# Gating values of a decoder trunk: token-major products of 256 columns become feature-major products with transposes

## The chip, the cores and the metric

One core of a Trainium2 chip runs the whole kernel in one launch. The metric is the device time of that core in microseconds, the median of several runs. One further run was taken with the profiler; all rows below come from it.

## The reference

The kernel computes one layer of a hybrid decoder for 2048 tokens of width 1024, all in float32. Cut to what the change touches:

```python
h = modulate(rms_norm(x, g_mix[l]), shift1, scale1)
proj = h @ w_in[l]                        # 1024 -> 2*512 (z_a: u|v) + 512 q + 128 k + 128 v
out_a = chunked_sgu(jax.nn.gelu(z_a), w_spatial[l], b_spatial[l])
out_b = sliding_window_sink_attention(q, k, v, sinks[l], positions)
x = x + gate1 * (concatenate([out_a, out_b], axis=-1) @ w_out[l])
...                                       # adaLN, squared-ReLU MLP of width 4096, final RMSNorm

def chunked_sgu(z, w_s, b_s):             # 8 groups x 64 channels, chunks of 128 tokens
    u, v = jnp.split(z, 2, axis=-1)
    v = v.reshape(B, n_chunks, CHUNK, GMLP_GROUPS, HEAD_DIM)
    w = w_s * causal[None]
    sv = jnp.einsum('hts,bcshd->bcthd', w, v) + jnp.transpose(b_s)[None, None, :, :, None]
    return u * sv.reshape(B, S, GMLP_WIDTH)
```

The gating contracts v over the tokens of a chunk, so its matmul wants v with tokens on the partitions. u only multiplies the result element by element, with features on the partitions.

## The kernel before

**Tiling.** The tokens are worked in four slabs of T = 512 (slab 0 to 3), D = 1024 in KT = 8 tiles of 128. Every product is made of float32r parts: an operand is split into a high part (a copy on ACT) and a low part (a subtraction on DVE), and a product is hi·hi + hi·lo + lo·hi, three matmuls per tile (`mm3`, L323 to L328). A projection of 128 output features for one slab is a `group` (L330): 8 tiles × 3 = 24 matmuls of 512 columns into one PSUM bank.

**Buffers.** PSUM has eight banks in four rings: `mm` (3 banks, the groups), `sc` (2: scores and the gating sums `so`), `pt` (2: transposes of attention and of v, and others), `ov` (1). In SBUF `wk` is a ring of 12 tiles of 128 × 1024 that holds weight blocks: raw weights, their high and low parts, and the MLP's tiles `w2w`, `w2h`, `w2l`, `aw`, `ah`, `al`.

**Weights.** `w_take` (L316) loads a weight block when it is first asked for; several keys load the next ones too. In slab 0 a block of `w_in` comes in raw (`raw`), ACT and DVE split it (L293, L294), and both parts are written to DRAM (`ki3h`, `ki3l` for block i3). Later slabs read those parts back (`whi<-ki2h`, `wlo<-ki2l`). All these transfers are issued by SP's queue in program order: writes are put in a list by `put` and sent when loads (`get`) come after them.

**The gating, `in_vu` (L514).** For a pair of feature tiles, `tokens(pp)` takes two weight blocks and makes v token-major: the 128 × 128 tile of h is the stationary operand and 256 weight columns are the moving one (L537 to L539), 4 token blocks × 8 tiles × 3 = 96 matmuls of 256 columns. Then come gelu on ACT (`vf`, L525), a copy to the high part (`vt`, L543) and a subtraction to the low part (L544). The u groups follow (24 matmuls of 512 columns each), then `gate(p)` (L548): 12 matmuls `so` on the parts of v (L557 to L559) and the additions on DVE (L562). The weight blocks are i0, i1 (v of p = 0, 1), i2, i3 (u0, u1), i4, i5 (v of p = 2, 3), i6, i7 (u2, u3). Each u group asks only for its own block.

**Order.** The program is written as generators that are woven together, and a scheduler unrolls it to one fixed order per engine. `in_vu` runs woven with the making of slab 1's h in slab 0; with slab 0's attention in slab 1; with `h2_build` (norm and MLP input of tokens of slabs 0 and 1) in slab 2; and as a side job of the first MLP pass `ffn_d(0)` (L1225 to L1251) in slab 3. In `Stat`, `finish` makes four column sums on TensorE (`msp`, L229), POOL and DVE make the diagonal factors `dg`, and `cast` spreads them with two matmuls `bcp` (L249), whose copy `rbc` (L251) starts the long DVE chain that makes h.

Of the kernel before, what the change touches and what calls it, by code (L numbers as in the profile page):

```python
# [11 lines left out]
F32 = mybir.dt.float32  # L12
F32R = mybir.dt.float32r
I32 = mybir.dt.int32
AF = mybir.ActivationFunctionType
ALU = mybir.AluOpType

P = 128
D = 1024
KT = D // P  # L20
# [3 lines left out]
NB = T // P  # L24
# [25 lines left out]
def hybrid_block(ctx, tc, x_l, c_l, pos, wada0, wada, vec, win, wsT, bs, sinks, wout, w1, w2, rope_c, y_l):  # L50
    nc = tc.nc
    pe, act, dve, pool = nc.tensor, nc.scalar, nc.vector, nc.gpsimd
# [4 lines left out]
    ps = ctx.enter_context(tc.tile_pool(name="ps", bufs=1, space=bass.MemoryType.PSUM))  # L57

    def t2(name, dt=F32, shape=None):
        return sb.tile(shape or [P, T], dt, name=name, tag="t2", bufs=NT)  # L60

    def m2(name, dt=F32R, shape=None):
        return sb.tile(shape or [P, T], dt, name=name, tag="m2", bufs=NM)
# [11 lines left out]
    def put(dst, out, in_):  # L75

        pend.append([0, dst, out, in_])
# [10 lines left out]
    def get(out, in_, src=None):  # L88

        known = [i for i, p in enumerate(pend) if p[1] is src]  # L90
        if src is not None and known:
            emit(known[-1] + 1)
        ins = nc.sync.dma_start(out=out, in_=in_)  # L93
        if not hold[0]:
            for p in pend:
                p[0] += 1
            emit(sum(p[0] > 1 for p in pend), ins)
        return ins
# [4 lines left out]
    def bank(tag="mm", name="mm"):  # L103
        return ps.tile([P, T], F32, name=name, tag=tag, bufs={"mm": 3, "sc": 2, "pt": 2, "ov": 1}[tag])


    ident = const.tile([P, P], F32, name="ident")
# [164 lines left out]
    last_mm = [None]  # L272
# [35 lines left out]
    def w_load(key):  # L308
        if key not in kept:
            return w_split(key)  # L310
        hi, lo = wk("whi"), wk("wlo")
        for t, d in zip((hi, lo), kept[key]):
            get(t.bitcast(F32), d, d)
        return Split([hi], [lo])

    def w_take(*keys):  # L316

        for key in keys:
            if key not in ready:
                ready[key] = w_load(key)  # L320
        return ready.pop(keys[0])

    def mm3(out, wh, wl, h, first, last, more=False):  # L323

        kw = dict(skip_group_check=True) if more else {}
        pe.matmul(out=out, lhsT=wh, rhs=h[0], start=first, stop=False, **kw)  # L326
        pe.matmul(out=out, lhsT=wh, rhs=h[1], start=False, stop=False, **kw)  # L327
        last_mm[0] = pe.matmul(out=out, lhsT=wl, rhs=h[0], start=False, stop=last, **kw)  # L328

    def group(rhs, *keys):  # L330
        w = w_take(*keys)
        out = bank()
        n = len(rhs)
        for k in range(n):
            mm3(out, *w.cut(k * P, (k + 1) * P), rhs[k], k == 0, k == n - 1)
        return out
# [177 lines left out]
    def in_vu(s, h, st, u0=None):  # L514
        vts, us = {}, {}
        sgu = list(wsp)
        if s > 0:
            ts = [m2("wsp", F32R, [P, 4, P]) for _ in range(4)]
            for t, d in zip(ts, wspd):
                get(t.bitcast(F32).rearrange("p g c -> p (g c)"), d, d)  # L520
            sgu = [ts[0:2], ts[2:4]]

        def gelu(bank, name):
            t = t2(name)
            act.activation(out=t, in_=bank, func=AF.Gelu_apprx_tanh)  # L525
            return t

        def tokens(pp):
            w = w_take(("i", 4 * pp), ("i", 4 * pp + 1)), w_take(("i", 4 * pp + 1))
            for half in range(2):  # L530
                o = bank()
                ov = o.rearrange("p (b c) -> p b c", b=2)
                for b in range(2):
                    cols = slice((2 * half + b) * P, (2 * half + b + 1) * P)
                    for k in range(KT):
                        hi, lo = w[k // 4].cut((k % 4) * 2 * P, (k % 4 + 1) * 2 * P)
                        pe.matmul(out=ov[:, b], lhsT=h[k][0][:, cols], rhs=hi, start=k == 0, stop=False)  # L537
                        pe.matmul(out=ov[:, b], lhsT=h[k][1][:, cols], rhs=hi, start=False, stop=False)
                        last_mm[0] = pe.matmul(out=ov[:, b], lhsT=h[k][0][:, cols], rhs=lo, start=False,  # L539
                                               stop=k == KT - 1)  # L540
                vf = gelu(o, "vf")
                vh, vl = m2("vt"), m2("vt")
                act.activation(out=vh, in_=vf, func=AF.Copy)  # L543
                dve.tensor_tensor(out=vl, in0=vf, in1=vh, op=ALU.subtract)  # L544
                vts[pp, half] = tuple(t.rearrange("p (b c) -> p b c", b=2) for t in (vh, vl))
                yield

        def gate(p):  # L548
            u = us.pop(p)
            sv = t2("sv")  # L550
            cols = slice((p % 2) * P, (p % 2 + 1) * P)
            w_h, w_l = (t[:, 2 * (p % 2):2 * (p % 2) + 2] for t in sgu[p // 2])
            for half in range(2):
                vh, vl = vts[p // 2, half]
                so = ps.tile([P, 2, 2, P], F32, name="so", tag="sc", bufs=2)
                for i in range(2):
                    pe.matmul(out=so[:, i], lhsT=vh[:, i, cols], rhs=w_h, start=True, stop=False)  # L557
                    pe.matmul(out=so[:, i], lhsT=vl[:, i, cols], rhs=w_h, start=False, stop=False)
                    pe.matmul(out=so[:, i], lhsT=vh[:, i, cols], rhs=w_l, start=False, stop=True)  # L559
                for hh in range(2):  # L560
                    r0, r1 = hh * HD, (hh + 1) * HD
                    dve.tensor_tensor(out=sv[r0:r1, half * 2 * P:(half + 1) * 2 * P].rearrange("p (c t) -> p c t", c=2),  # L562
                                      in0=so[r0:r1, :, hh, :],
                                      in1=bsb[r0:r1, p, :].unsqueeze(1).broadcast_to([HD, 2, P]), op=ALU.add)
            dve.tensor_tensor(out=sv, in0=sv, in1=u, op=ALU.mult)
            put(mixd[s][p], mixd[s][p], sv)

        for pp in range(2):
            for _ in tokens(pp):
                if pp and 1 in us:  # L570
                    gate(1)
                yield
            for p in (2 * pp, 2 * pp + 1):
                us[p] = u0 if p == 0 and u0 is not None else gelu(group(h, ("i", 4 * (p // 2) + 2 + p % 2)), "u")
                if p % 2:
                    gate(p - 1)
                if p > 0 or u0 is None:
                    yield
        gate(3)
        yield  # L580


# [550 lines left out]
    h, fed = [], [0] * NPRE  # L1133
# [27 lines left out]
    with tc.issue_after(ahead[0].ins):  # L1161
        setup_mixers()
        rope_load(0)
        st = sts[0]
        va_rest = do_va(0, bva, st)
        u0 = t2("vf")
        act.activation(out=u0, in_=bv0, func=AF.Gelu_apprx_tanh)
        va_rest()
        do_k(0, bk, st)
        for j, b in enumerate((bq0, bq1, bq2, bq3)):  # L1170
            do_q(0, j, b, st)
        rb, hn = [], []
        ada = chain(ada_rest(2), ada_rest(3), ada_rest(4))
        weave(in_vu(0, h, st, u0), chain(x_stats(1, rb), spread(rb), h_build(1, rb, hn)), per=2)
# [19 lines left out]
    def then_halo(s, g):  # L1194
# [5 lines left out]
    st1 = sts[1]  # L1200
    mix, mix1, rn, hx = [], [], [], []
    weave(chain(in_qkv(1, hn, st1), in_vu(1, hn, st1)),
          ratio(chain(then_halo(0, attention(0, st)), mix_build(0, mix)), 3,
                chain(part(ada, 6), x_stats(2, rn), spread(rn)), 1), per=3.5)
# [8 lines left out]
    next(h2)  # L1213
    next(h2)
    weave(in_vu(2, hx, sts[2]), h2, per=1.5)
    run(h2)
    w2f, ada = w2_early(), ada_rest(5)
# [98 lines left out]
```

## Time and profile before

| | before |
|---|---|
| runs, median (lowest to highest) | 2097.52 us (2090.8 to 2101.14), 3 runs |
| the profiled run, its span | 2087.11 us, 2085.4 us |
| TensorE (PE) busy | 1917.2 us (92%), 8852 matmuls |
| VectorE (DVE) busy | 1419.1 us (68%) |
| ScalarE (ACT) busy | 914.2 us (44%) |
| main DMA queue | 67.5% of 16 engines' span |
| mean granted PE clock | 0.967 |

The profiled run is 10.4 us below the median of the runs shown. PE, DVE, ACT, POOL and SP are the engines; PEld is TensorE's loading of the stationary operand, which lies beside its matmuls. SPq is the queue on SP that issues transfers. In a row of the timeline the bracket tells how long the engine sat idle before the instruction and what released it. Consecutive matmuls overlap in the pipe, so what one costs in a stream is the distance between starts, not its recorded duration.

### The profile page before, as it was taken

To read this page: it belongs to the slowest core of one execution; us is meant where nothing else is said; L and a number is where in the kernel's file an instruction comes from. 1 tells how busy PE (TensorE), PEld (TensorE's weight loads), DVE (VectorE), ACT (ScalarE), POOL (GpSimd) and SP (SyncE) were. 2 spreads that over 40 slices of the span, in tenths; PEclk is the share of its full clock that TensorE was granted. 3 is DMA by queue.
4 is the path that set the end of the run, shared out by engine and by line. 5 is a ranking of instruction groups with operands and counts; after the bars stand their busy time and mean duration, and the time that the engine had idled before them with its cause. 6 is when DMAs were issued, how large, how long until landed. Compare 5 with 4: busy or idle time off the path is not lost.

```text
span 2085.4 us, 25949 instructions
## 1 busy us (share of the span) xinstructions
PE 1917.2 (92%) x8852; PEld 1581.0 (76%) x8852; DVE 1419.1 (68%) x2400; ACT 914.2 (44%) x1565; POOL 170.9 (8%) x234
## 2 busy tenths in 40 slices
PE   5899898988999999889979979989999999999997
PEld 4788776777877788668867757767888888888875
DVE  8578789648776765784565675794766665544674
ACT  3435644334443444633443344543454444433442
POOL 4301312100000000110101120000000000000000
PEclk9999999999999999889989999999999999999998
DMA  9797497982577857797577778675444446556663
GB/s 318 295 354 249 146 347 236 356 324 101 202 270 249 268 174 247 249 323 254 204 271 248 241 261 313 237 257 162 172 152 162 155 153 208 193 200 210 234 214 129
DMA packets 236214, 486.77 MB, mean 233 GB/s; under 512 B 23809, under 2 KB 81281, under 8 KB 236081
## 3 DMA queue, kind: packets, MB, share of 16 engines
q1 hardware_dynamic: 234960, 484.38, 67.5%
q8 instruction: 70, 1.15, 0.2%
q0 software_dynamic: 1120, 0.72, 0.1%
q14 instruction: 64, 0.52, 0.1%
HBM read 349.55 MB, written 135.46 MB: 233 GB/s over the span
## 4 chain that ended last, share of the span: by engine, by line
PE 47%; DMA 9%; DVE 6%; ACT 2%; issue 1%; SPq 1%; POOL 0%; POOLq 0%; DVEq 0%; ACTq 0%
PE mm L327 15%; PE mm L328 15%; PE mm L326 15%; DMA aw<-ad 3%; DMA xt<-in_x_dram 1%; DVE al L70 1%; DMA w2w<-in_w_dram 1%; DMA xt<-x2d 1%; ACT ah L69 1%; DVE w2l L70 1%; DMA w2w<-w2d 1%; DMA xt<-mixb 1%; SPq L93 1%; DVE x L950 1%; DMA w2d<-a 1%
## 5 line engine op out<-in xcount | busy, mean ns | idle before, releaser
L327 PE MATMUL mm<-al,w2h 128*128 128x512 f32 x896 | 356.0, 397 | 12.6 <-DVE al L70 12.2
L328 PE MATMUL mm<-ah,w2l 128*128 128x512 f32 x896 | 352.9, 394 | 0.0
L326 PE MATMUL mm<-ah,w2h 128*128 128x512 f32 x896 | 313.8, 402 | 24.8 <-ACT ah L69 21.4
L69 ACT ACTIVATE w2h<-w2w 128x1024 fp32r<-128x1024 f32 x112 | 118.6, 1059 | 306.4 <-DMA w2w<-w2d 151.2
L70 DVE TENSOR_TENSOR w2l<-w2w,w2h 128x1024 fp32r<-128x1024 f32 x112 | 137.5, 1227 | 168.7 <-ACT w2h L69 160.4
L326 PEld LDWEIGHTS mm<-ah,w2h 128*128 128x128 f32 x896 | 171.1, 193 | 64.3 <-ACT ah L69 25.6
L327 PEld LDWEIGHTS mm<-al,w2h 128*128 128x128 f32 x896 | 171.2, 191 | 56.9 <-DVE al L70 21.9
L328 PEld LDWEIGHTS mm<-ah,w2l 128*128 128x128 f32 x896 | 171.0, 191 | 35.3
L70 DVE TENSOR_TENSOR al<-aw,ah 128x1024 fp32r<-128x1024 f32 x112 | 137.6, 1228 | 37.7 <-ACT ah L69 30.5
L69 ACT ACTIVATE ah<-aw 128x1024 fp32r<-128x1024 f32 x112 | 118.5, 1058 | 65.6 <-DMA aw<-ad 33.7
L326 PE MATMUL mm<-h,whi 128*128 128x512 f32 x320 | 126.1, 406 | 9.7 <-ACT h L264 6.1
L327 PE MATMUL mm<-h,whi 128*128 128x512 f32 x320 | 128.3, 402 | 1.6 <-DVE h L265 1.6
L234 POOL TENSOR_TENSOR rs<-ms,mhalf 128x4 f32<-128x4 f32 x12 | 17.7, 1473 | 1355.1 <-DVE ms L232 1342.3
L328 PE MATMUL mm<-h,wlo 128*128 128x512 f32 x320 | 127.6, 399 | 1.2 <-DVE wlo L294 1.2
L326 PE MATMUL mm<-mix,whi 128*128 128x512 f32 x256 | 103.5, 407 | 20.9 <-ACT mix L703 11.8
L326 PE MATMUL mm<-hw,wah 128*128 128x512 f32 x256 | 101.4, 398 | 10.3 <-ACT p L889 9.5
L327 PE MATMUL mm<-mix,whi 128*128 128x512 f32 x256 | 103.1, 403 | 1.3 <-DVE mix L704 1.3
L328 PE MATMUL mm<-mix,wlo 128*128 128x512 f32 x256 | 101.8, 398 | 0.0
L326 PE MATMUL mm<-hw,wdh 128*128 128x512 f32 x256 | 99.8, 390 | 2.2 <-DVE w L912 2.2
L327 PE MATMUL mm<-hw,wah 128*128 128x512 f32 x256 | 100.9, 394 | 0.0
L328 PE MATMUL mm<-hw,wal 128*128 128x512 f32 x256 | 100.5, 394 | 0.0
L326 PE MATMUL mm<-hw,wbh 128*128 128x512 f32 x256 | 99.7, 389 | 0.0
(258 smaller groups left out, 4293.7 us busy)
## 6 DMA issues: line engine op xcount, KB each, us to landing
aw<-ad SPq DMA_DIRECT2D x112, 512.0 KB, 4.9
r<-in_w_dram SPq DMA_DIRECT2D x64, 512.0 KB, 5.0
w2w<-w2d SPq DMA_DIRECT2D x64, 512.0 KB, 3.6
a<-in_w_dram SPq DMA_DIRECT2D x96, 256.0 KB, 4.3
ad<-wt SPq DMA_DIRECT2D x96, 256.0 KB, 2.2
w2w<-in_w_dram SPq DMA_DIRECT2D x96, 256.0 KB, 3.6
xt<-in_x_dram SPq DMA_DIRECT2D x80, 256.0 KB, 5.1
adar<-in_wada_dram SPq DMA_DIRECT2D x32, 512.0 KB, 6.8
```

Source lines behind the costliest of these rows:

```text
L69: act.activation(out=hi, in_=t, func=AF.Copy)
L70: dve.tensor_tensor(out=lo, in0=t, in1=hi, op=ALU.subtract)
L93: ins = nc.sync.dma_start(out=out, in_=in_)
L234: self.pow = pool.tensor_tensor(out=rs[:, :nb], in0=ms[:, :nb], in1=mhalf[:, :nb], op=ALU.pow)
L326: pe.matmul(out=out, lhsT=wh, rhs=h[0], start=first, stop=False, **kw)
L327: pe.matmul(out=out, lhsT=wh, rhs=h[1], start=False, stop=False, **kw)
L328: last_mm[0] = pe.matmul(out=out, lhsT=wl, rhs=h[0], start=False, stop=last, **kw)
L950: dve.scalar_tensor_tensor(out=xs[r, t, b], in0=src, scalar=mod[:, 5 * KT + 4 * r + b:5 * KT + 4 * r + b + 1], in1=xs[r, t, b], op0=ALU.mu ...
```

## The change

v is made like every other projection: for each feature tile p, 24 matmuls of 512 columns (`mm3`) give v with features on the partitions. gelu goes to SBUF as before. `turn(p)` then makes four 128 × 128 transposes on TensorE into one `pt` bank (`vq`, L532 after), and the copy and the subtraction that split v (L534, L535 after) read that bank instead of SBUF. A short list `todo` puts each `turn` and each `gate` behind the next group. The weight blocks are asked for one ahead: the second v block brings the first u block with it, and a u group brings the block after it.

```diff
-        def tokens(pp):
-            w = w_take(("i", 4 * pp), ("i", 4 * pp + 1)), w_take(("i", 4 * pp + 1))
...
-                        pe.matmul(out=ov[:, b], lhsT=h[k][0][:, cols], rhs=hi, start=k == 0, stop=False)
-                        pe.matmul(out=ov[:, b], lhsT=h[k][1][:, cols], rhs=hi, start=False, stop=False)
-                        last_mm[0] = pe.matmul(out=ov[:, b], lhsT=h[k][0][:, cols], rhs=lo, start=False,
...
-                vf = gelu(o, "vf")
-                vh, vl = m2("vt"), m2("vt")
-                act.activation(out=vh, in_=vf, func=AF.Copy)
-                dve.tensor_tensor(out=vl, in0=vf, in1=vh, op=ALU.subtract)
...
+        def turn(p):
+            vf = vts.pop(p)
+            vp = ps.tile([P, NB, P], F32, name="vq", tag="pt", bufs=2)
+            for b in range(NB):
+                pe.transpose(out=vp[:, b], in_=vf[:, b * P:(b + 1) * P], identity=ident)
+            vh, vl = m2("vt", F32R, [P, NB, P]), m2("vt", F32R, [P, NB, P])
+            act.activation(out=vh, in_=vp, func=AF.Copy)
+            dve.tensor_tensor(out=vl, in0=vp, in1=vh, op=ALU.subtract)
+            vts[p] = vh, vl
...
+        todo = []
+
+        def behind():
+            while todo:
+                f, p = todo.pop(0)
+                f(p)
+
         for pp in range(2):
-            for _ in tokens(pp):
-                if pp and 1 in us:
-                    gate(1)
+            two = w_take(("i", 4 * pp), ("i", 4 * pp + 1)), w_take(("i", 4 * pp + 1), ("i", 4 * pp + 2 + (pp == 0 and u0 is not None)))
+            for p in (2 * pp, 2 * pp + 1):
+                o = bank()
+                for k in range(KT):
+                    c = (k % 4) * 2 * P + (p % 2) * P
+                    mm3(o, *two[k // 4].cut(c, c + P), h[k], k == 0, k == KT - 1)
+                vts[p] = gelu(o, "vf")
+                behind()
+                todo.append((turn, p))
                 yield
             for p in (2 * pp, 2 * pp + 1):
-                us[p] = u0 if p == 0 and u0 is not None else gelu(group(h, ("i", 4 * (p // 2) + 2 + p % 2)), "u")
-                if p % 2:
-                    gate(p - 1)
-                if p > 0 or u0 is None:
+                if p == 0 and u0 is not None:
+                    us[p] = u0
+                else:
+                    us[p] = gelu(group(h, ("i", 4 * pp + 2 + p % 2), ("i", min(4 * pp + 3 + p % 2, 7))), "u")
+                    behind()
                     yield
-        gate(3)
+                todo.append((gate, p))
+        behind()
```

**SP in slab 0.** Here `raw` is a raw block of `w_in`; before, `raw_1146` is block i3 and the two after it are i4 and i5. Rows with `ki` are writes of split parts to DRAM. Before:

```order
L86 DMA wsp2_872<-wsh_868 128x512
L86 DMA wsp3_873<-wsl_869 128x512
L86 DMA ki0l_960<-wlo_956 128x1024
L86 DMA ki1h_991<-whi_987 128x1024
L86 DMA ki1l_992<-wlo_988 128x1024
L93 DMA raw_1146<-in_win_dram 128x1024
L93 DMA raw_1210<-in_win_dram 128x1024
L93 DMA raw_1218<-in_win_dram 128x1024
L86 DMA ki3h_1152<-whi_1148 128x1024
```

And with the change, where `raw_993` is block i3 and `raw_1109` is i4:

```order
L86 DMA wsp2_872<-wsh_868 128x512
L86 DMA wsp3_873<-wsl_869 128x512
L93 DMA raw_993<-in_win_dram 128x1024
L86 DMA ki0h_959<-whi_955 128x1024
L86 DMA ki0l_960<-wlo_956 128x1024
L86 DMA ki1h_991<-whi_987 128x1024
L86 DMA ki1l_992<-wlo_988 128x1024
L86 DMA ki3h_1001<-whi_997 128x1024
L93 DMA raw_1109<-in_win_dram 128x1024
```

The load of i3 has moved ahead of three writes that stood before it; the load of i4 now stands behind the write of i3's high part, which waits for that part to be made on ACT.

**PE in slab 2**, from the column sums of `h2_build` to its first spreading matmul. Before:

```order
L328 MATMUL mm<-h,wlo 128x512
L229 MATMUL msp<-ones,ssum 128x1 x4
L249 MATMUL bcp<-dg,ones_r 128x512
L326 MATMUL mm<-h,whi 128x512
L327 MATMUL mm<-h,whi 128x512
```

And with the change:

```order
L229 MATMUL msp<-ones,ssum 128x1 x4
L326 MATMUL mm<-h,whi 128x512
L327 MATMUL mm<-h,whi 128x512
L328 MATMUL mm<-h,wlo 128x512
L249 MATMUL bcp<-dg,ones_r 128x512
L532 MATMUL vq<-ident,vf 128x128 x4
L326 MATMUL mm<-h,whi 128x512
```

The second `bcp` stood 20 matmuls of 512 columns behind the first; now four transposes and 16 such matmuls lie between them. From the start of slab 2's v, the sums stood behind 96 matmuls of 256 and 24 of 512 columns; now they stand behind 69 of 512 columns.

**SP in slab 3**, beside `ffn_d(0)`. `w2w` and `aw` are the raw halves of the MLP's second-layer work, in the `wk` ring; `ki2` and `ki3` are the u blocks of slab 3. Before:

```order
L86 DMA mixb_139<-os 64x4x128
L93 DMA w2w<-w2d_3_209 128x1024
L93 DMA aw<-ad_6_3_265 128x1024
L86 DMA kd_8990<-kr 128x512
L93 DMA whi<-ki2h 128x1024
L93 DMA wlo<-ki2l 128x1024
L86 DMA vd_9034<-vf 128x512
```

And with the change:

```order
L86 DMA mixb_139<-os 64x4x128
L93 DMA whi<-ki2h 128x1024
L93 DMA wlo<-ki2l 128x1024
L86 DMA kd_8762<-kr 128x512
L93 DMA w2w<-w2d_3_209 128x1024
L93 DMA aw<-ad_6_3_265 128x1024
L86 DMA vd_8806<-vf 128x512
L93 DMA whi<-ki3h 128x1024
```

The u block is asked for ahead of the MLP's tile, so that tile takes ring buffers that come free later. Counted in the order of PE, from the matmul that frees its buffer to the first one that uses it, the tile `w2d_3_209` had 49 matmuls of 512 and 56 of 256 columns between (with 8 of 128); with the change 27 and 8 (with 8 of 128). For the next three tiles with the change it is 33 and 6 (with 8 transposes), 33 and 6 (with 4), and 25 and 10 (with 4); for the second one before it was 32 and 19.

## Rows read from the trace of the kernel before

**Rows 1.** Page: busy time, share of the span and instructions of each engine
```profile
PE 1917.2 (92%) x8852; PEld 1581.0 (76%) x8852; DVE 1419.1 (68%) x2400; ACT 914.2 (44%) x1565; POOL 170.9 (8%) x234
```

**Rows 2.** Windows, slabs 0, 2, 3: length, busy PE, PEld, DVE, ACT, POOL, PE clock, DMA, GB/s
```profile
75.00:112.00 37.00, 31.03 (x222) 29.47 (x221) 26.76 (x45) 22.20 (x39) 4.07 (x9) 0.95 0.73 260
456.00:506.00 50.00, 40.86 (x226) 35.86 (x225) 47.95 (x81) 26.42 (x46) 0.00 (x0) 0.88 0.40 133
960.00:1035.00 75.00, 74.52 (x445) 66.38 (x446) 37.50 (x81) 29.96 (x54) 5.37 (x8) 1.00 0.71 239
```

**Rows 3.** Timeline, PE, 256 columns at full clock: start, duration, instruction (first, last of 47)
```profile
77.65 0.28 PE L538 MATMUL mm<-whi,h 128*128 128x256 f32 x1
...
83.17 0.28 PE L539 MATMUL mm<-wlo,h 128*128 128x256 f32 x1
```

**Rows 4.** Timeline, PE, 512 columns at full clock (first and last of 40)
```profile
417.28 0.39 PE L328 MATMUL mm<-mix,wlo 128*128 128x512 f32 x1
...
426.12 0.39 PE L328 MATMUL mm<-mix,wlo 128*128 128x512 f32 x1
```

**Rows 5.** Timeline, PE: four transposes of v, and two of attention among other matmuls
```profile
75.55 0.60 PE L490 MATMUL vp<-ident,va 128*128 128x128 f32 x4
...
173.79 0.38 PE L652 MATMUL tpp<-ident,pr 128*128 128x128 f32 x2
173.93 0.37 PE L537 MATMUL mm<-whi,h 128*128 128x256 f32 x1
174.13 0.38 PE L652 MATMUL tpp<-ident,pr 128*128 128x128 f32 x2
```

**Rows 6.** By line: duration ns least/median/most of splitting v, and of attention's from PSUM
```profile
L543 ACT ACTIVATE vt<-vf x16: 612/624/635, 106.7 to 1018.5; 128x512 fp32r<-128x512 f32 x16
L654 ACT ACTIVATE pc<-tpp x32: 574/597/607, 171.1 to 1227.5; 128x512 fp32r<-128x512 f32 x32
L544 DVE TENSOR_TENSOR vt<-vf,vt x16: 674/684/693, 108.6 to 1019.7; 128x512 fp32r<-128x512 f32 x16
L655 DVE TENSOR_TENSOR pc<-tpp,pc x32: 661/686/693, 171.7 to 1228.1; 128x512 fp32r<-128x512 f32 x32
```

**Rows 7.** Timeline, slab 0: PE, ACT and the queue on SP around 80 us
```profile
88.13 0.58 PE L537 MATMUL mm<-whi,h 128*128 128x256 f32 x1 [4.68 <-ACT qf L430]
...
91.07 0.40 PE L538 MATMUL mm<-whi,h 128*128 128x256 f32 x1
...
86.53 1.06 ACT L293 ACTIVATE whi<-raw 128x1024 fp32r<-128x1024 f32 x1 [6.86 <-DMA raw<-in_win_dram]
87.50 1.55 ACT L430 ACTIVATE qf<-mm 128x512 f32<-128x512 f32 x3
...
77.36 0.90 SPq L86 DMA_DIRECT2D ki0l<-wlo  x1
...
79.83 2.94 SPq L93 DMA_DIRECT2D raw<-in_win_dram  x3
```

**Rows 8.** Page, DMA issues: KB of each, us from issue to landing
```profile
r<-in_w_dram SPq DMA_DIRECT2D x64, 512.0 KB, 5.0
```

**Rows 9.** Timeline, PE, slab 1: the longest wait
```profile
243.45 0.58 PE L557 MATMUL so<-wsp,vt 128*128 128x256 f32 x1 [3.64 <-ACT vt L543]
```

**Rows 10.** Timeline, PE, slab 2: the first spreading matmul, and the first to use `wch`
```profile
448.74 0.47 PE L249 MATMUL bcp<-dg,ones_r 128*128 128x512 f32 x1 [3.10 <-DVE dg L243]
...
501.11 0.79 PE L326 MATMUL mm<-hw,wch 128*128 128x512 f32 x1 [4.40 <-ACT wch L69]
```

**Rows 11.** Timeline, slab 3: issue of two tiles `w2w` on SP, splitting on ACT and DVE
```profile
1013.73 0.32 SPq L93 DMA_DIRECT2D w2w<-w2d  x1
...
1020.33 1.22 DVE L70 TENSOR_TENSOR al<-aw,ah 128x1024 fp32r<-128x1024 f32 x1
...
1025.44 0.36 SPq L93 DMA_DIRECT2D w2w<-w2d  x1
...
1033.10 1.06 ACT L69 ACTIVATE ah<-aw 128x1024 fp32r<-128x1024 f32 x1 [1.29 <-DVE w2l L70]
```

More of the change, by code (lines that the diff above doesn't have):

```diff
@@ L526, in gelu @@
             return t
-        def tokens(pp):
-            w = w_take(("i", 4 * pp), ("i", 4 * pp + 1)), w_take(("i", 4 * pp + 1))
[L530 to L536, printed above, removed]
-                        pe.matmul(out=ov[:, b], lhsT=h[k][0][:, cols], rhs=hi, start=k == 0, stop=False)
-                        pe.matmul(out=ov[:, b], lhsT=h[k][1][:, cols], rhs=hi, start=False, stop=False)
-                        last_mm[0] = pe.matmul(out=ov[:, b], lhsT=h[k][0][:, cols], rhs=lo, start=False,
-                                               stop=k == KT - 1)
-                vf = gelu(o, "vf")
-                vh, vl = m2("vt"), m2("vt")
-                act.activation(out=vh, in_=vf, func=AF.Copy)
-                dve.tensor_tensor(out=vl, in0=vf, in1=vh, op=ALU.subtract)
-                vts[pp, half] = tuple(t.rearrange("p (b c) -> p b c", b=2) for t in (vh, vl))
-                yield
@@ L548, in gate @@
+        def turn(p):
[7 more added lines that the diff above has]
+            vts[p] = vh, vl
         def gate(p):
-            u = us.pop(p)
+            u, (vh, vl) = us.pop(p), vts.pop(p)
@@ L550, in gate @@
             sv = t2("sv")
-            cols = slice((p % 2) * P, (p % 2 + 1) * P)
             w_h, w_l = (t[:, 2 * (p % 2):2 * (p % 2) + 2] for t in sgu[p // 2])
             for half in range(2):
-                vh, vl = vts[p // 2, half]
                 so = ps.tile([P, 2, 2, P], F32, name="so", tag="sc", bufs=2)
                 for i in range(2):
-                    pe.matmul(out=so[:, i], lhsT=vh[:, i, cols], rhs=w_h, start=True, stop=False)
-                    pe.matmul(out=so[:, i], lhsT=vl[:, i, cols], rhs=w_h, start=False, stop=False)
-                    pe.matmul(out=so[:, i], lhsT=vh[:, i, cols], rhs=w_l, start=False, stop=True)
+                    b = 2 * half + i
@@ L560, in gate @@
+                    pe.matmul(out=so[:, i], lhsT=vh[:, b], rhs=w_h, start=True, stop=False)
+                    pe.matmul(out=so[:, i], lhsT=vl[:, b], rhs=w_h, start=False, stop=False)
+                    pe.matmul(out=so[:, i], lhsT=vh[:, b], rhs=w_l, start=False, stop=True)
                 for hh in range(2):
```

## The prediction

> **What bounds the kernel now.** I read the page first. TensorE is busy for 92% of the span [rows 1], so over most of the time it is the bound, and the change is worth what it takes from TensorE's stream plus what it does to TensorE's waits. v and u of the gating are made once per slab, in four short places, so the second view is the windows around three of them [rows 2], and the fourth is read in the timeline. In slab 0 TensorE is busy 31.03 of 37 us. In slab 2 DVE is busy 47.95 of 50 us and TensorE 40.86, with a granted clock of 0.88: there DVE is the bound. In slab 3 TensorE is busy 74.52 of 75 us: it has nothing to gain but its own work, and every wait that appears is a loss. Slab 1 is woven with attention, and its longest wait is for the high part of v [rows 9]. The third view is the timeline of those places, for the price of one matmul and for what ends each wait.
>
> **The stream on TensorE.** Removed: 768 matmuls of 256 columns (192 per slab). In the stream the 47 of [rows 3] start (83.17 - 77.65) / 46 = 0.120 us apart, so they take 768 x 0.120 = 92.2 us. Added: 384 of 512 columns; the 40 of [rows 4] start (426.12 - 417.28) / 39 = 0.2267 us apart, so 87.0 us. That saves 5.1 us, 1.3 per slab. Twice the columns cost 1.89 times as much, and that little is all that the shape gives.
>
> Added: 64 transposes. Four of v in a row are recorded with 0.60 us together [rows 5]. In the stream, two of attention and one matmul of 256 columns take 174.13 - 173.79 = 0.34 us, so a transpose takes (0.34 - 0.12) / 2 = 0.11. 64 x 0.11 = 7.0 us, 1.8 per slab. Net +0.5 us per slab. In slabs 0, 1 and 3 this lies on TensorE's path: +1.4. In slab 2 it is covered by DVE's chain and costs nothing as long as TensorE still waits 4.40 us at that chain's end [rows 10].
>
> The Trainium skill speaks against the transposes: "TensorE: Matmul & The Clock Gate", Part 4 (PE-mode transpose), tells of about 275 ns for one of them in a kernel's context, most of it access latency. By that the 64 would cost 17.6 us in place of 7.0. The trace shows such a time as the recorded length of one, and not as its price in a stream, where starts lie 0.11 us apart.
>
> **Splitting v.** 16 copies and 16 subtractions stay, and now read PSUM. The nearest rows are attention's, which read PSUM: 597 against 624 ns on ACT, 686 against 684 on DVE [rows 6]. Nothing changes by more than 0.5 us in all, off TensorE's path. But their result is now two steps later: group, gelu, transposes, copy. The queue of work behind the next group (5.4 us) covers this where ACT has no backlog.
>
> **Slab 0, the load of i3.** Before, TensorE stops for 4.68 us at 88.13 [rows 7]. It waits for a bank that the copy `qf` frees; that copy stands on ACT behind the splitting of i3, and ACT waited 6.86 us for its transfer. i3 is issued at 79.83 behind three writes and lands at 86.5, 6.7 us later. With the change it stands ahead of these writes, at the place of the one issued at 77.36. It lands 5.0 us [rows 8] to 6.7 us later: at 82.4 to 84.1, in place of 86.5. TensorE restarts 1.6 us behind the landing (88.13 - 86.53), so at 84.0 to 85.7, against the end of its group at 83. The gain is 2.4 to 4.1 us. After the wait, 13 steps take 91.07 - 88.13 = 2.94 us, at 13 x 0.120 = 1.56 at full clock: 1.4 us lost at the lower of the two clocks, which I count as saved with most of the wait. So 2.4 to 5.5; I take 5.0, nearer the upper end, since the writes that shared the DMA engines now come later. Against it: the load of i4 now stands behind the write of i3's high part, and on ACT the gelu of the first v group stands behind the splitting of i4, so the first `vq` may wait some 1 us (0 to 2.4). Net -4.0 (bounds -5.5 to 0).
>
> **Slab 1.** The same chain remains: softmax work, change of ACT's table, gelu, copy, then the gating. `vq` shares two `pt` banks with attention's transposes, which can add a wait; the gating comes one group later, which can take one away. The only price is the wait of 3.64 us that is there [rows 9]: bounds -3 to +3, and I take 0.
>
> **Slab 2.** The column sums stand behind 69 x 0.2267 = 15.6 us of matmuls in place of 96 x 0.120 + 24 x 0.2267 = 17.0: 1.3 us earlier. The first `bcp` waits for `dg` as before (3.10 us [rows 10], less three matmuls). The second comes 4 x 0.11 + 16 x 0.2267 = 4.1 us after it in place of 4.5. So the copy `rbc` and the DVE chain behind it start 1.7 us earlier, and as DVE has no idle time to the end of the chain [rows 2], `wch` comes as much earlier. I take -2.0 with the clock, bounds -4 to +1: v's own split has to wait on ACT behind `rbc`, and a wait of TensorE there is covered up to the 4.40 us.
>
> **Slab 3.** The u blocks now take ring buffers ahead of the MLP's tiles, so each of four tiles has less TensorE work between the release of its buffer and its first use: by the counts with the order, 7.8, 9.1, 8.6 and 7.3 us, where the first had 18.6 before. A tile needs from issue to its last part 1020.33 + 1.22 - 1013.73 = 7.8 us, or, with a landing that is late, 1033.10 + 1.06 + 1.22 - 1025.44 = 9.9 us [rows 11]. The shortfall is 0.5 us in all at the first and 2.1 + 0.8 + 1.3 + 2.6 = 6.8 us at the second. I take +1.5, nearer the first, since it is DMA's usual pace there.
>
> **Sum.** +1.4 - 4.0 + 0 - 2.0 + 1.5 = -3.1 us against the profiled run, 2087.1 to 2084.0. That run lies 10.4 us below the median shown, so for the median of runs: 2097.5 - 3.1 = 2094.4 us. A measurement of this kernel can tell about 0.5%, 10.5 us, from no change.
>
> **The rivals.**
> (a) The waits go and nothing new comes: slab 0 gives 5.5, slab 1 gives 3, slab 2 gives 4, slab 3 costs nothing, +1.4 for the stream: -11.1, 2086.4 us. For it: every wait named is real and ends in a chain that the change shortens. Against: slabs 1 and 2 have the next chain (ACT's backlog, DVE) right behind.
> (b) The `wk` ring becomes the bound in slab 3: the upper shortfall of 6.8 us, and after each of four waits a stretch at the lower clock as in slab 0, 4 x 1.4 = 5.6. That is +12.4 in place of +1.5: 2094.4 + 10.9 = 2105.3 us, slower than before; with slab 0 giving nothing, 2109. It decides where issue to last part takes over 8 us. For it: TensorE has 0.5 us of slack in 75. Against: one of the two tiles shown needs less than that, and the first use wants the high parts alone.
> (c) Each transpose of `vq` costs its whole length, because it waits for the one before to leave the array: four take 0.60 us with three steps of 0.11 [rows 5], so one is 0.60 - 0.33 = 0.27 long. 48 outside slab 2 x (0.27 - 0.11) = +7.7, 2102.1 us. Against: four transposes of v stand in a row in [rows 5], and they overlap. This is the case of the Trainium skill's page above, "TensorE: Matmul & The Clock Gate".
> (d) The change only swaps one shape for another and its early loads come to nothing, because DMA is full there: +1.4, or 2098.9 us. For it: i3 could land late all the same, behind what is already under way at 77 us.
>
> **How the numbers follow.** The forecast 0.45, (a) 0.20, (b) 0.20, (c) 0.05, (d) 0.10. The range takes (a) and (b) in, with the spread of the runs shown (2090.8 to 2101.1, some 5 us to each side) around the ends: 2080 to 2111. Faster by over 0.5%, below 2087: half of (a), a sixth of the forecast (bounds of slabs 0 to 2 together) and some of what I have not seen, 0.25. Slower by over 0.5%, above 2108: half of (b) and a tenth of the rest, 0.17. The rest is 0.58.
>
> **What would show it.** In the profile after: 512-column matmuls in place of L537 to L539 at 0.227 us spacing and `vq` at 0.11; `raw` issued near 77.4 and a wait of TensorE near 83 of 1 to 2 us instead of 4.68; in slab 2 `rbc` about 2 us earlier against the start of the slab and the wait at `wch` still there; in slab 3 waits for `ah` or `w2h` of 0 to 3 us each. The prediction is wrong if slab 3's windows show TensorE with more than 5 us of waits, if transposes cost over 0.2 us in the stream, or if slab 1 moves by more than 3 us.

## The result, and the profile after

The change made the kernel slower: 2110.6 us median (2107.31 to 2114.63, 6 runs) against 2094.16 us (2085.46 to 2101.14, 6 runs) of the kernel before beside it. The ratio is 1.0081, with an interval of 1.006 to 1.0102. The forecast was 2094.4 us and no change that can be told; 2110.6 lies at the upper edge of its range, and the time moved the other way than forecast. The profiled run of after took 2109.38 us, its span is 2107.7 us, and its mean granted clock is 0.961. One execution of 6681.61 us, among those of the kernel with tiles on POOL's queue below, is left out of that kernel's median and ratio.

TensorE's work changed as counted. On the page of after:

```profile
PE 1933.6 (92%) x8532; PEld 1574.3 (75%) x8532; DVE 1419.1 (67%) x2400; ACT 916.1 (43%) x1567; POOL 169.3 (8%) x234
```

Against [rows 1], 320 matmuls are gone (768 less 384 and 64). Busy time is nevertheless 16.4 us higher. The recorded durations of matmuls overlap, so this number does not say what the shapes cost. What matters are the starts and the waits. The costliest groups on the page of after tell more, in their last column (idle time ahead of the group, and what ended it):

```profile
L326 PE MATMUL mm<-ah,w2h 128*128 128x512 f32 x896 | 313.5, 404 | 38.1 <-ACT ah L69 34.9
```

The same group on the page of before:

```profile
L326 PE MATMUL mm<-ah,w2h 128*128 128x512 f32 x896 | 313.8, 402 | 24.8 <-ACT ah L69 21.4
```

So 13.5 us more are ended by `ah`, the high parts of the MLP's tiles, which the diff does not touch. Over the whole span this is only a hint: a second profile of before has 28.0 us in place of 21.4, and two more of after have 29.7 and 26.8. Where the loss lies has to be read by stages.

**Where the time went.** Both traces were cut at the same TensorE instructions. A to B: first column sums `msp` to the first `mm<-hw,wah` (slabs 0 to 2). B to C: on to the first `mm<-ah,w2h` (first part of the first MLP pass). C to D: to the 65th of these. D to E: to the 129th (slab 3's gating lies there). E to F: to the end. Distances in us:

| profiled run | A to B | B to C | C to D | D to E | E to F | span |
|---|---|---|---|---|---|---|
| before | 477.1 | 332.8 | 87.9 | 134.9 | 1040.8 | 2085.4 |
| before, once more | 478.5 | 334.2 | 88.0 | 136.6 | 1049.0 | 2097.8 |
| after | 475.9 | 338.7 | 86.5 | 145.6 | 1048.9 | 2107.7 |
| after, once more | 473.1 | 337.1 | 89.0 | 146.2 | 1041.9 | 2099.2 |
| after, third | 471.7 | 340.2 | 87.6 | 144.6 | 1045.6 | 2101.2 |

The means of after less those of before are -4.2, +5.2, -0.3, +9.7 and +0.6 us. The last stage differs by 8 us between two executions of one kernel, so a single profile against a single profile (22.3 us here) says too much. Two stages lose in every profile: slab 3 most (D to E), and the first part of the first MLP pass (B to C).

**Slab 3**, in the windows of after (columns as in [rows 2]):

```profile
960.00:1029.00 69.00, 61.96 (x294) 50.37 (x292) 25.41 (x55) 23.41 (x45) 5.41 (x8) 0.98 0.68 226
1029.00:1045.00 16.00, 15.08 (x66) 12.72 (x67) 8.95 (x18) 7.13 (x10) 0.00 (x0) 0.87 0.43 145
```

Where TensorE was busy 74.52 of 75 us [rows 2], it now lacks 7 of 69, and the mean clock from 1029 on is 0.87. The wait is in TensorE's timeline of after:

```profile
1029.92 2.08 PE L326 MATMUL mm<-ah,w2h 128*128 128x512 f32 x4 [5.71 <-ACT ah L69]
1031.80 0.41 PE L546 MATMUL so<-wsp,vt 128*128 128x256 f32 x1
...
1032.87 0.41 PE L548 MATMUL so<-wsp,vt 128*128 128x256 f32 x1
```

And the window just behind the wait:

```profile
1029.90:1034.00 4.10, 4.08 (x14) 3.57 (x15) 2.77 (x6) 4.02 (x6) 0.00 (x0) 0.59 0.00 0
```

This is the fourth of the four tiles. The five steps of 256 columns from 1031.80 to 1032.87 are 0.21 us apart, against 0.12 in [rows 3]: the lower of the two clock levels, granted 0.50 from 1029.90 to 1032.90. The tile view of `ah` for this stretch sums 7.7 us of TensorE's waits in three places, where that of before has none. The clock had already fallen during the long wait, where it costs nothing (0.69 over 1024.30 to 1029.90, with TensorE idle). Behind the wait it is 0.59 over 4.10 us, which costs 1.7 us. Together that is 9.4 of the 145.6 - 134.9 = 10.7 us between these two profiles, and the stream's +0.5 per slab belongs to the rest.

Why that tile is late is read in TensorE, SP's queue, DVE and ACT of after:

```profile
1016.73 0.39 PE L328 MATMUL mm<-h,wlo 128*128 128x512 f32 x1
...
1016.95 0.32 SPq L93 DMA_DIRECT2D s<-w2d  x1
1020.16 0.32 SPq L93 DMA_DIRECT2D xt<-mixa  x1
1020.53 0.76 SPq L93 DMA_DIRECT2D w2w<-w2d  x1
1021.34 0.42 SPq L93 DMA_DIRECT2D aw<-ad  x1
...
1019.44 0.69 DVE L832 TENSOR_TENSOR a<-a,s 128x512 f32<-128x512 f32 x1 [5.25 <-DMA s<-w2d]
...
1024.91 1.06 ACT L69 ACTIVATE w2h<-w2w 128x1024 fp32r<-128x1024 f32 x1 [14.36 <-DMA w2w<-w2d]
1025.98 1.28 ACT L641 ACT_TABLE_LOAD   x1
...
1028.83 1.04 ACT L69 ACTIVATE ah<-aw 128x1024 fp32r<-128x1024 f32 x1
```

The matmul at 1016.73 is the last on block i4, whose buffer the tile takes: it is free at 1016.9. The load is issued at 1020.53 only. On SP `xt` stands ahead of it in the program's order; `xt` goes out at 1020.16, once the addition on DVE (L832) that started at 1019.44 is done, and DVE had waited for `s`, itself issued at 1016.95. In the other two profiles of after the load goes out 3.3 and 3.8 us behind the release, with the same two transfers ahead. `w2w` lands at 1024.8. Then ACT has a softmax group of the attention (from 1025.98) between `w2h` and `ah`. From release to the end of `ah` that makes 13 us, and TensorE had 7.3 us of work for it, as counted.

**Slabs 0 to 2** gave 4.2 us. The wait of 4.68 us [rows 7] is gone, as the timeline of after shows (SP's issue of i3, TensorE's one wait left there, and ACT):

```profile
72.65 0.64 SPq L93 DMA_DIRECT2D raw<-in_win_dram  x1
...
79.94 0.50 PE L326 MATMUL mm<-h,whi 128*128 128x512 f32 x1 [1.29 <-ACT qf L430]
...
82.08 1.05 ACT L293 ACTIVATE whi<-raw 128x1024 fp32r<-128x1024 f32 x1
83.04 1.06 ACT L430 ACTIVATE qf<-mm 128x512 f32<-128x512 f32 x2
```

The column sums of the next slab start at 110.83 in place of 116.54 (5.7, 7.3 and 7.6 us earlier in the three profiles). By the following sums the lead is 2.0, 5.1 and 3.9 us only. In slab 1 the wait of [rows 9] is gone, but TensorE waits longer for a bank that the gelu of v frees, where before has 1.78 us at 202.5:

```profile
198.12 0.79 PE L326 MATMUL mm<-h,whi 128*128 128x512 f32 x1 [3.13 <-ACT vf L525]
```

Slab 2's chain starts earlier, as forecast, and its two waits of [rows 10] are shorter in this profile; in the other two of after the first is 1.91 us again, but the second 4.23 and 4.81, so that one did not shrink:

```profile
446.23 0.77 PE L249 MATMUL bcp<-dg,ones_r 128*128 128x512 f32 x1 [1.90 <-DVE dg L243]
...
497.82 0.79 PE L326 MATMUL mm<-hw,wch 128*128 128x512 f32 x1 [2.89 <-ACT wch L69]
```

**The first MLP pass** has two long waits in after that are short in before (0.83 us for `u` at 719.0, 1.02 us for `p` at 720.7):

```profile
718.72 0.47 PE L326 MATMUL mm<-hw,wah 128*128 128x512 f32 x1 [3.03 <-DVE u L926]
...
742.97 0.65 PE L326 MATMUL mm<-hw,wah 128*128 128x512 f32 x1 [3.56 <-ACT p L893]
```

### The profile page after: what moved, and what is told of

Its sections match the earlier page's. It is cut to its first block, busy times and chain, and to the rows that moved or that the text cites. A ratio compares the mean times of both kernels' runs of the same rounds, so it can differ in the third digit from the quotient of the medians.

```text
span 2107.7 us, 25306 instructions
## 1 busy us (share of the span) xinstructions
PE 1933.6 (92%) x8532; PEld 1574.3 (75%) x8532; DVE 1419.1 (67%) x2400; ACT 916.1 (43%) x1567; POOL 169.3 (8%) x234
## 4 chain that ended last, share of the span: by engine, by line
PE 40%; DMA 9%; DVE 6%; ACT 3%; issue 2%; SPq 1%; POOL 0%; POOLq 0%; DVEq 0%; ACTq 0%
PE mm L327 13%; PE mm L328 13%; PE mm L326 13%; DMA w2w<-in_w_dram 2%; DMA aw<-ad 2%; DMA w2w<-w2d 1%; DVE al L70 1%; DVE w2l L70 1%; DMA w2d<-a 1%; SPq L93 1%; DMA xt<-in_x_dram 1%; ACT ah L69 1%; ACT w2h L69 1%; DVE x L954 1%; DMA xt<-mixb 1%
## 5 line engine op out<-in xcount | busy, mean ns | idle before, releaser
L326 PE MATMUL mm<-h,whi 128*128 128x512 f32 x448 | 182.0, 414 | 17.2 <-ACT h L264 6.2
L327 PE MATMUL mm<-h,whi 128*128 128x512 f32 x448 | 181.7, 406 | 3.4 <-DVE h L265 3.4
L328 PE MATMUL mm<-h,wlo 128*128 128x512 f32 x448 | 181.5, 405 | 1.8 <-DVE wlo L294 1.2
L326 PE MATMUL mm<-mix,whi 128*128 128x512 f32 x256 | 103.1, 407 | 16.0 <-ACT mix L707 12.9
L326 PEld LDWEIGHTS mm<-h,whi 128*128 128x128 f32 x448 | 88.4, 198 | 39.0 <-ACT h L264 7.0
L327 PEld LDWEIGHTS mm<-h,whi 128*128 128x128 f32 x448 | 88.7, 198 | 23.0 <-DVE h L265 5.6
L328 PEld LDWEIGHTS mm<-h,wlo 128*128 128x128 f32 x448 | 87.8, 196 | 20.9 <-DVE wlo L294 1.6
```

## The experiments

Two theories stood at the start. Theory 1: asking for the u blocks ahead takes ring buffers from the MLP's tiles, and the loss is in slab 3. Theory 2: the way of v is longer, by the transposes and their split. The expectations below also speak of a third, that asking ahead costs as much in slabs 1 and 2 through another order. In the diffs, `two` and `group` are the two places of the change that ask for blocks.

**The change without asking ahead.**

```diff
-            two = w_take(("i", 4 * pp), ("i", 4 * pp + 1)), w_take(("i", 4 * pp + 1), ("i", 4 * pp + 2 + (pp == 0 and u0 is not None)))
+            two = w_take(("i", 4 * pp), ("i", 4 * pp + 1)), w_take(("i", 4 * pp + 1))
...
-                    us[p] = gelu(group(h, ("i", 4 * pp + 2 + p % 2), ("i", min(4 * pp + 3 + p % 2, 7))), "u")
+                    us[p] = gelu(group(h, ("i", 4 * pp + 2 + p % 2)), "u")
```

> The change without the asking ahead: the second v block and the u groups ask for their own weight block alone. Theory 1 (the u blocks that are asked for ahead take buffers of the wk ring, and the MLP's tiles come late in slab 3): the waits for ah between 985 and 1030 us (1.5 + 0.5 + 5.7 and some 3 us of lower clock) go, slab 0's wait for i3 comes back (4.7 us), so 11 to 15 us less than the change and 5 to 8 more for slab 0: about 2094 to 2102 where the change takes 2110.6. Theory 2 (the longer way from group over gelu, transposes and copy to the gating, with transposes in the pt banks, costs the time): 2106 to 2115, with the waits of slab 3 still there.

Measured: 2095.03 us against 2094.35, ratio 1.0006 (0.999 to 1.0021). The other shape with its transposes is no change by itself, and Theory 2 falls as the cause. Its stages are 474.4, 332.3, 85.4, 136.3 and 1053.7 us: neither of the two losses is there. The last stage is 8.8 us above the mean of before, which is about what two executions of before differ in it; whether the shape has a part in it is not shown. A to B is 3.4 us shorter than before with no early load at all. By these profiles the early load of i3 has only about 1 us in the 4.2 that slabs 0 to 2 gained, and most of the lead that it wins in slab 0 is lost again on the way. (A stage of a single profile is known to a few us only.)

**Asking ahead in the kernel before**, in token-major form.

```diff
-            w = w_take(("i", 4 * pp), ("i", 4 * pp + 1)), w_take(("i", 4 * pp + 1))
+            w = w_take(("i", 4 * pp), ("i", 4 * pp + 1)), w_take(("i", 4 * pp + 1), ("i", 4 * pp + 2 + (pp == 0 and u0 is not None)))
...
-gelu(group(h, ("i", 4 * (p // 2) + 2 + p % 2)), "u")
+gelu(group(h, ("i", 4 * (p // 2) + 2 + p % 2), ("i", min(4 * (p // 2) + 3 + p % 2, 7))), "u")
```

> The kernel before with the asking ahead and nothing else of the change: token-major v stays. Theory 1: slab 0 gains 5 to 6 us, slab 3 loses some 8 to 14, about 2096 to 2106. Theory 2: only the gain in slab 0, about 2086 to 2091.

Measured: 2088.92 us, ratio 0.9968 (0.9956 to 0.998). Theory 1 in its first form is wrong: asking ahead alone makes the kernel faster. Run once more on another chip:

> The kernel before with the asking ahead in all slabs, timed again: 0.2 to 0.45% under before, 2083 to 2089 where before takes 2092, if the first comparison holds.

2085.59 us, ratio 0.9979 (0.9964 to 0.9995). Its slab 3 (D to E) takes 136.3 and 134.6 us, like before. The order says why. Between release and first use the fourth tile keeps 36 matmuls of 512 columns and 23 of 256, as before: 36 x 0.2267 + 23 x 0.120 = 10.9 us. With the change it is 25 and 10 with four transposes, 7.3 us. Only the second tile waits here, 1.78 and 1.06 us. So the loss of slab 3 needs both parts of the change.

**Asking ahead in some slabs only**, in the kernel after: both places get the condition `s == 0`, `s < 3` or `s == 3`.

```diff
-w_take(("i", 4 * pp + 1), ("i", 4 * pp + 2 + (pp == 0 and u0 is not None)))
+w_take(("i", 4 * pp + 1), *([("i", 4 * pp + 2 + (pp == 0 and u0 is not None))] if s == 0 else []))
```

> The change, asking ahead in slab 0 alone. Theory 1: the gain in slab 0 stays and slab 3's waits go: 11 to 15 us less than the change, 2096 to 2100, about the time of before. Theory 2: within 3 us of the change, 2108 to 2113.

> The change, asking ahead in slabs 0, 1 and 2 and not in slab 3. Theory 1 (short cover of the MLP's tiles in slab 3): as with the asking ahead in slab 0 alone, 2096 to 2101. Theory 3 (the asking ahead in slabs 1 and 2 costs as much as that in slab 3, over another order of the work after it): 2104 to 2111.

> The change, asking ahead in slab 3 alone. Theory 1: the 2095 of the change without asking ahead and 9 to 13 us more, 2104 to 2108, with the waits for ah in slab 3 again. Theory 3: 2094 to 2098.

Measured: slab 0 alone 2098.02 us, ratio 1.001 (0.9996 to 1.0025); slabs 0 to 2 2094.76, 1.0022 (1.0006 to 1.0038); slab 3 alone 2096.05, 1.0033 (1.0015 to 1.005). The stages of their profiles tell more than the totals:

| profiled run | A to B | B to C | C to D | D to E | E to F | span |
|---|---|---|---|---|---|---|
| slab 0 alone | 474.7 | 338.8 | 89.1 | 138.3 | 1043.8 | 2096.5 |
| slabs 0 to 2 | 469.2 | 337.4 | 87.9 | 139.1 | 1043.6 | 2089.7 |
| slab 3 alone | 474.6 | 332.6 | 85.5 | 146.9 | 1046.1 | 2098.0 |

Slab 3's loss of some 10 us is there when u blocks are asked for ahead in slab 3, and only then; the first two runs keep some 3 us over before, with a wait for the gelu of v of 1.7 and 1.9 us. In the third the wait is TensorE's again, with the same releaser:

```profile
1021.82 1.65 PE L326 MATMUL mm<-ah,w2h 128*128 128x512 f32 x3 [5.99 <-ACT ah L69]
```

Between slab 0 alone and slabs 0 to 2 the ratios overlap, so asking ahead in slabs 1 and 2 costs nothing that can be told, and the third theory falls. But slab 3 alone gives only about half of the 0.4 to 0.6% that Theory 1 wanted: 2096.05 us misses its 2104 to 2108 and even lies in the third theory's range, though before was 3.4 us faster on this chip than beside that kernel. D to E does hold the whole loss, 10.6 us over the kernel without asking ahead; the last stage is 7.6 us shorter, within what two executions differ. Another part of the change's loss hangs on slab 0: as soon as slab 0 asks ahead in the feature-major kernel, B to C takes 337 to 341 us in place of 327 to 333. (In the token-major kernel it takes 334 to 336 with asking ahead, against 333 and 334 before.) No run of the change shows this loss without asking ahead in slab 0, none with it lacks it. Nothing in that stage's source differs. The order that the scheduler writes there does, and DVE's timeline of after shows it ahead of the wait of 3.03 us:

```profile
711.94 0.69 DVE L816 TENSOR_TENSOR a<-a,a 128x512 f32<-128x512 f32 x1 [4.67 <-DMA a<-in_w_dram]
...
713.15 1.21 DVE L70 TENSOR_TENSOR wal<-r,wah 128x1024 fp32r<-128x1024 f32 x1
...
717.90 0.68 DVE L926 TENSOR_TENSOR u<-mm,u 128x512 f32<-128x512 f32 x1
```

And the same place without asking ahead:

```profile
707.34 1.23 DVE L70 TENSOR_TENSOR wal<-r,wah 128x1024 fp32r<-128x1024 f32 x1 [3.15 <-ACT wah L69]
708.52 0.69 DVE L739 TENSOR_TENSOR wt<-b,p 128x512 f32<-128x512 f32 x1
709.12 0.69 DVE L865 TENSOR_TENSOR s<-r 128x512 f32<-128x512 f32 x1
709.73 0.69 DVE L926 TENSOR_TENSOR u<-mm,u 128x512 f32<-128x512 f32 x1
```

There `u` starts 2.4 us behind the start of `wal`, with two additions between. In after it starts 4.75 us behind it, and DVE had stood 4.67 us for a transfer just ahead. That this order makes the loss is argued from the rows, and not shown: in before `u` starts 6.2 us behind `wal` (711.95 and 718.13), and TensorE waits only 0.83 us for it. Putting the old order back in that place alone was not tried.

**The change again, twice.**

> The change, once more, for a second profile of it. If the waits of slab 3 belong to the order of its instructions, they stand again: TensorE waits some 1.5 us, 0.5 us and 4 to 7 us for ah between 985 and 1035 us, with a stretch of lower clock behind the last one; if they were chance, the last is under 2 us. The two waits of 3 us near 719 and 743 us stand again (they were there in the run with the asking ahead in slab 0 alone, and not in the other two).

> The change itself, timed beside the next three on the same chip. 2105 to 2112 if the first measurement holds here too; the three profiles of this order so far lose 8.7 to 10.0 us between the tiles 6 and 7 of the MLP's product in slab 3.

2100.88 us against 2090.97 in one run, then 2102.29 against 2089.56, ratio 1.0063 (1.0042 to 1.0085). The forecast of 2105 to 2112 was missed: the change costs less on these chips, and before is faster there too. The loss of slab 3 stands in both profiles, with waits of 5.87 and 5.34 us at the same place.

**The kernel before again**, for what one profile is worth.

> The kernel before, once more, for a second profile of it: how far its stalls and the times of its stages differ from one execution to the next. Every theory: the waits at 83 to 88 us (4.7 us) and in slab 2 stand again within 0.5 us; in the first MLP pass (540 to 820 us) the waits for p, w and u may differ by some us; the span lies between 2085 and 2100.

2099.55 us, span 2097.8: 12.4 us above the span of the profiled run of before, with nothing changed. The waits in slabs 0 and 2 stand again (4.46, 3.10 and 4.37 us).

**Each transpose three times**, without asking ahead. It adds 128 transposes and changes nothing else in the source.

```diff
-            for b in range(NB):
+            for b in [*range(NB)] * 3:
```

> The change without asking ahead, and each of the 64 transposes made three times into the same place: 128 transposes more, 96 of them outside slab 2. At 0.11 us each and on TensorE's path outside slab 2: 10.6 us more than the 2095 of that run, 2104 to 2108. If one costs its recorded length of 0.27 us: 26 us more, 2121. If transposes lie in time that TensorE waits anyway: within 3 us of 2095.

Measured: 2097.26 us, ratio 1.0025 (1.0006 to 1.0044), so 0.19% or some 4 us above the kernel without asking ahead, though the two intervals overlap. By the stream the 96 outside slab 2 should have given 10.6 us. The timeline has twelve in a row:

```profile
99.53 1.47 PE L532 MATMUL vq<-ident,vf 128*128 128x128 f32 x12
100.75 0.48 PE L326 MATMUL mm<-h,whi 128*128 128x512 f32 x1
101.07 0.39 PE L327 MATMUL mm<-h,whi 128*128 128x512 f32 x1
```

From 99.53 to 101.07, less one matmul of 0.227, is 1.31 us for twelve: 0.109 each. At the 0.27 of rival (c), 96 would cost 26 us; that falls. The median lies within 3 us of 2095, the forecast for transposes in time that TensorE waits anyway. The stages of the profile do not bear that out: against the kernel without asking ahead A to B is 12.9 us longer (487.3) and D to E 3.3 (139.6), while B to C is 4.9 shorter (327.4). That profile is of the slowest of the twelve runs, so why less than 10.6 us arrives in the median stays open.

**In slab 3 the first two u blocks ahead only** (i2 and i3; i6 and i7 as before the change).

```diff
-w_take(("i", 4 * pp + 1), ("i", 4 * pp + 2 + (pp == 0 and u0 is not None)))
+w_take(("i", 4 * pp + 1), *([("i", 4 * pp + 2 + (pp == 0 and u0 is not None))] if s < 3 or pp == 0 else []))
...
-group(h, ("i", 4 * pp + 2 + p % 2), ("i", min(4 * pp + 3 + p % 2, 7)))
+group(h, ("i", 4 * pp + 2 + p % 2), *([("i", min(4 * pp + 3 + p % 2, 7))] if s < 3 or pp == 0 and not (s == 3 and p % 2) else []))
```

> The change, but in slab 3 only the first two u blocks (i2, i3) are asked for ahead, i6 and i7 not. The counts of matmuls between release and first use of the four tiles become 27 of 512, 45, 73 and 45, where the change has 27, 33, 33 and 25. Theory 1: the wait of 5.9 us at the fourth tile and the lower clock behind it go, 7 to 10 us less than the change on this chip. Theory 3 (the order of the rest costs it): within 3 us of the change.

Measured: 2104.04 us, ratio 1.0065 (1.0042 to 1.0088), no better than the change where Theory 1 expected 7 to 10 us less; D to E is 142.7, only some 3 us less. The fourth tile, for which TensorE has 45 matmuls of 512 columns and 16 of 256 ahead here, does not wait any more. Yet the second, whose own first use comes without a wait at 994.84, now holds up something else. TensorE's and ACT's timelines:

```profile
985.66 0.79 PE L326 MATMUL mm<-h,whi 128*128 128x512 f32 x1 [4.16 <-ACT vf L525]
986.25 0.63 PE L327 MATMUL mm<-h,whi 128*128 128x512 f32 x1
986.68 0.63 PE L328 MATMUL mm<-h,wlo 128*128 128x512 f32 x1
...
982.64 1.06 ACT L69 ACTIVATE w2h<-w2w 128x1024 fp32r<-128x1024 f32 x1 [7.91 <-DMA w2w<-w2d]
983.72 1.28 ACT L525 ACT_TABLE_LOAD   x1
985.01 0.60 ACT L525 ACTIVATE vf<-mm 128x512 f32<-128x512 f32 x1
```

TensorE waits for a bank that the gelu of v frees. The gelu stands on ACT behind the splitting of that tile, and ACT stands 7.91 us until the tile lands. So a tile can cost TensorE before its own first use too, through ACT's order; the expectation had priced only the first use.

**Tiles by another queue.** In the kernel after, `w2w` and `aw` of the product's tiles 4 to 8 are issued on POOL's queue. The four late tiles are numbers 4 to 7 of these.

```diff
-                    get(wraw, w2d[i, c], w2d[i, c])
-                get(araw, ad[p, i, c])
+                    get(wraw, w2d[i, c], w2d[i, c], pool if p == 0 and i == 6 and c > 2 else None)
+                get(araw, ad[p, i, c], None, pool if p == 0 and i == 6 and c > 2 else None)
```

> The change, with the loads of the MLP's tiles 4 to 8 of the product in slab 3 (w2w and aw) issued from POOL's queue in place of SP's; the order of PE and the counts of matmuls between release and first use stay. In the change the fourth late tile's buffer came free at 1016.89 and SP issued it at 1020.53, 3.6 us later, behind a load of the side work that waited for another landing. Theory 1a (SP's order holds the tile): it is issued within 1 us of its release, the wait of 5.3 to 5.9 us falls to about 2, and the whole to 1.003 to 1.006 of before, where the change has 1.0063 to 1.0081. Theory 1b (the buffer itself comes too late and the landing is slow): the wait stays at 4 us or more.

Measured: 2097.0 us against 2091.53, ratio 1.0027 (1.0009 to 1.0045), better than the change by 0.4 to 0.5%; D to E falls to 139.3. POOL's timeline shows the load of the fourth late tile going out when TensorE frees the buffer, with nothing ahead of it:

```profile
1019.66 0.55 POOL L93 DMA_DIRECT2D w2w<-w2d  x1 [6.11 <-PE mm L328]
```

This fits an SP queue that holds the tile up, but it does not show it cleanly. The schedule moved with the edit, against what the expectation said: the fourth tile then had 48 matmuls of 512 columns ahead of its first use in place of 25, and did not wait at all. How much of the 6 us is the queue and how much the longer cover stays open.

**What beats both kernels: token-major, asking ahead in slabs 0 to 2**, on the idea that asking ahead gains in slab 0 and loses in slab 3. Beside the edit to the kernel before shown above, both places get `if s < 3`.

> The kernel before, asking ahead in slabs 0 to 2 and not in slab 3: the tiles' cover in slab 3 is that of before (wait of 1.8 us at the second tile gone). Theory 1: 1 to 3 us under the run with asking ahead in all slabs. If the asking ahead in slab 3 does not matter to the token-major order: the same within 1 us.

Measured: 2080.21 us against 2089.56, ratio 0.9957 (0.994 to 0.9974): 9 us faster than before. Set against the two ratios of after (1.0063 and 1.0081), it is 1.1 to 1.2% faster than the change. Its stages are 467.2, 336.4, 87.7, 136.2 and 1036.9 us: A to B is 10.6 us below the mean of before, and slab 3 is as it was. Against asking ahead in all slabs it is 5.4 us faster where 1 to 3 were expected, with intervals that overlap. The reason given does not hold for that: D to E is 136.2 us here and 136.3 and 134.6 there, so what more it gains does not come from slab 3, and its cause is open.

## Why the prediction was wrong

- **The stream: right.** TensorE's v matmuls in after start at 90.27, 90.50, 90.72 and so on to 92.31: nine steps in 2.04 us, 0.227 each. Four `vq` start at 101.63 and the matmul after the next at 102.30, so (0.67 - 0.227) / 4 = 0.111 for a transpose, as from [rows 4, 5]. The kernel without asking ahead measures the sum: 1.0006. The Trainium skill's 275 ns ("TensorE: Matmul & The Clock Gate", Part 4) appears as the recorded length of one `vq`, 272 ns in the median, and not as its price.
- **Slab 0: right in kind, larger in size at first.** i3 was issued at 72.65, earlier than forecast, and the wait went. The column sums came 5.7 to 7.6 us earlier, against -4.0 net with an end at -5.5. Little of it reached the end of slab 2: A to B is 473.6 us in the mean of after and 474.4 without any asking ahead.
- **Slab 1: wrong in sign.** Taken as 0 (bounds ±3). By the next column sums 2.2 to 3.7 us of the lead were given back in the three profiles; the wait for `vf` of 3.13 us, on ACT's backlog, is one place of it. In two of the three that is over the 3 us named as a sign of being wrong.
- **Slab 2: right.** `rbc` starts at 452.69 in place of 455.68, so 3.0 us earlier, of which 1.7 were forecast by its own steps. The wait at `wch` is still there. The four terms for slabs 0 to 2 were together about -5; the traces show -4.2. That they agree is luck: the forecast had too small a gain in slab 0 and no loss in slab 1, and the two errors cancel.
- **Slab 3: the failed step.** The term was "+1.5, nearer the first, since it is DMA's usual pace there". It measured +9.7. The covers were counted right (7.3 us for the fourth tile). What a tile needs was not: the prediction measured it from the issue on, and took the quicker of two tiles (7.8 us, the other 9.9). The fourth tile took 9.3 us from its issue to the end of `ah`, 2.9 of them softmax that the scheduler puts between the two copies on ACT, and before its issue it stood 3.6 us behind other transfers on SP, which no term held. The need must be counted from the release of the buffer: 13 us. Rows of before, where tiles had longer cover, could not show what that order would be. Its bound, 6.8, was passed by the waits alone (7.7), and the lower clock behind the long wait added 1.7. This is rival (b), given 0.20. It expected four short waits, and one long one did most of it.
- **Unforeseen: the first MLP pass, +5.2.** The prediction let everything outside the four slabs keep its order. With the scheduler that did not hold, and the place lies 600 us behind slab 0, with whose early load it comes and goes. What in the new order makes the loss is open.
- **"If slab 3's windows show TensorE with more than 5 us of waits"** was the stated sign of failure, and that is what the windows show.

-4.2 + 5.2 - 0.3 + 9.7 + 0.6 = +11.0 us by the means of the profiles; the medians say +16.4 and, on another chip, +12.7, and a single run on a third +9.9. Single profiles of one kernel differ by as much as the difference.

## What to carry to other kernels

Count the cover of a load from the release of its buffer to its first use, and set against it the whole way: what stands ahead in the issuing queue, the landing, and what stands between on the engine that prepares it. A load that is asked for earlier in a shared ring can make another one later: here asking ahead in slab 3 cost some 10 us in the feature-major order, where the fourth tile kept 7.3 us of cover, and nothing that can be told in the token-major one, where it kept 10.9. So try an early load apart from the change of shape, and stage by stage: token-major with asking ahead in slabs 0 to 2 gave 0.43%. Under a scheduler compare the order of the whole program, not only of the stage that was edited.

## What was unexpected in the hardware

- Two executions of the kernel before differ by 12.4 us in span (2085.4 and 2097.8), 8.2 of it in the last stage, so a stage of a single profile is known here to a few us at best.
- Behind one wait of 4.16 us TensorE's matmuls of 512 columns start 0.43 us apart (986.25, 986.68), at a granted clock of 0.50 from 986 to 988, the lower of the two levels. In after the clock fell within the wait of 5.71 us, and the 4.10 us behind it ran at 0.59 in the mean. One long wait therefore cost more than its length, there by 1.7 us.
